# A two-layer hybrid decoder trunk: the pre-norm's factor moved behind the products, and transposed products turned to tokens on the partitions

## The chip, the core and the metric

One Trainium2 chip, one of its cores. The metric is the device time of one execution in microseconds (us). The kernel before took 1545.32 us, the median of 3 runs (1544.34 to 1547.5).

## What is computed

Two layers (D = 1024, 256 tokens, FFN width 2816) on a residual x in float32. Cut to what matters here:

```python
for l in range(DEPTH):
    x = x + 0.5 * rmsnorm(swiglu(rmsnorm(x, ffn1_pre_g[l]), w_ffn1_in[l], w_ffn1_out[l]), ffn1_post_g[l])
    h = rmsnorm(x, mix_pre_g[l])
    (z, xbc, dt_raw, rq, rk, rv, rg, aq, ak, av, gate) = split(h @ w_in[l])
    ys = [ssd_mixer(z, xbc, dt_raw, ...), retention_mixer(rq, rk, rv, rg, ...), swa_sink_attention(aq, ak, av, ...)]
    y = sum(sigmoid(gate + b_gate[l])[m] * (ys[m] @ w_branch[l, m]) for m in range(3)) @ w_out[l]
    x = x + rmsnorm(y, mix_post_g[l])
    x = x + 0.5 * rmsnorm(swiglu(rmsnorm(x, ffn2_pre_g[l]), w_ffn2_in[l], w_ffn2_out[l]), ffn2_post_g[l])
# rmsnorm(x, g) = x * rsqrt(mean(x * x) + EPS) * g; swiglu: silu(a) * b, then w_out
```

## The kernel before

Six phases run one after the other: FFN, mixer, FFN, for each layer. Every operand of a large product is held as two fp32r tiles, the rounded value (hi) and what is left (lo), and each product is three matmuls (`mm3`, lines 87 to 89): hi by lo, hi by hi, lo by hi. The weights are read in tiles of 128 x 1024 (512 KB, `raw`, 4 buffers) by SP's queue and split by ScalarE (hi, line 67) and VectorE (lo, line 68) into `hl`, 8 buffers, two of the eight 128-row blocks of a chunk in each; a chunk is 512 columns of a weight.

A product comes in two forms. `gemm` (line 91) keeps a block of the activations in TensorE, transposed (xT, yT, hT, with features on the partitions), and streams 512 columns of weights: the result has 128 tokens on the partitions. `gemmT` (line 100) keeps 128 columns of the weight and streams 256 tokens: the result has features on the partitions, which is how the next product wants it. It serves FFN chunks 2 to 10, the convolution's input `xbc`, the gates and the branch products. FFN chunks 0 and 1 use `gemm` and are transposed by TensorE.

Between two phases (a joint, in the prediction) `close` makes the last product for token tiles 0 and 1 (t = 0, 1), `postnorm` updates x, and `prenorm` opens the next phase: the sum of squares on ScalarE (line 135), two steps on GpSimd for the factor r (lines 126 and 128), xn = x * r * g on VectorE (line 161), eight transposes per tile (line 146) into PSUM (`pst`, 3 banks), and the split into hi and lo halves of xT. The engines run their queues in order; the order on each is set by the scheduler of the tile layer, from a model of its own of the times. Inside the mixer, `pump` hands out the small steps of attention, retention and the state-space scan between the products.

Of the kernel before, what the change touches and what calls it, by code (L numbers as in the profile page):

```python
# [11 lines left out]
ALU = mybir.AluOpType  # L12
# [27 lines left out]
class Trunk:  # L40
# [59 lines left out]
    def gemmT(self, ps, xT, slots, c0):  # L100
        """the transposed product: 128 columns of the weight from c0 on, by all tokens"""
        for k, (wh, wl) in enumerate(slots):
            x = xT[k // 2]
            cs = slice(c0, c0 + P)
            self.mm3(ps, wh[:, cs], wl[:, cs], x[:, k % 2, 0], x[:, k % 2, 1], k == 0, k == len(slots) - 1)

    def swiglu(self, a, b):
        nc = self.nc
        sl = self.t1([256], name="sl")
        nc.scalar.activation(out=sl, in_=a, func=AF.Silu)  # L110
        h = self.t1([256], name="h")
        nc.vector.tensor_tensor(out=h, in0=sl, in1=b, op=ALU.mult)  # L112
        return h
# [9 lines left out]
    def rstd(self, ss, eps):  # L123
# [143 lines left out]
    def begin(self, gname, l):  # L267
        """norm and transposes that open a phase: returns the tiles and what does one token tile"""
        g = self.gain(gname, l)
        xT = self.new_T(4, "xT")  # L270
        return xT, lambda t: self.prenorm(xT, t, g)
# [4 lines left out]
    def close(self, order, gemm, gpost, scale, nxt):  # L276
        """output projection, residual update and the next phase's opening, token tile by token tile"""
        y = {}
        for n, t in order:
            y[t, n] = gemm(n, t)  # L280
            if n:
                self.postnorm(t, [y[t, 0], y[t, 1]], gpost, scale, 4 * EPS, nxt is None)
                if nxt:
                    nxt(t)

    def ffn(self, i, l, xT, nxt):
        nc, A = self.nc, self.A
        w = A[f"w_ffn{i}_in"][l]
# [34 lines left out]
    def att_kv(self, t, ps):  # L323
# [22 lines left out]
    def att_q(self, g, t, ps):  # L346
# [3 lines left out]
        nc.scalar.activation(out=qn[:, :, 0], in_=ps, func=AF.Copy, scale=0.125)  # L350
        nc.vector.scalar_tensor_tensor(out=qn[:, :, 1], in0=ps, scalar=0.125, in1=qn[:, :, 0].bitcast(F32),
# [73 lines left out]
    def rotate(self, key, t, ps):  # L425
# [5 lines left out]
        nc.vector.tensor_tensor(out=a, in0=ps, in1=cs[:, 0].unsqueeze(1).unsqueeze(1).to_broadcast([P, 4, 2, 64]),  # L431
                                op=ALU.mult)
        for o in range(2):
            nc.vector.tensor_tensor(out=b[:, :, o], in0=ps[:, :, 1 - o],
                                    in1=cs[:, 1 + o].unsqueeze(1).to_broadcast([P, 4, 64]), op=ALU.mult)
# [75 lines left out]
    def silu2(self, ps, dtype=F32, name="gz"):  # L511
        """2 * silu of a PSUM bank, in a new SBUF tile"""
        nc = self.nc
        g = self.t2([512], name=name)
        nc.scalar.activation(out=g, in_=ps, func=AF.Tanh, scale=0.5)
        nc.vector.scalar_tensor_tensor(out=g, in0=g, scalar=1.0, in1=ps, op0=ALU.add, op1=ALU.mult)
        return g

# [37 lines left out]
    def conv(self, i, ps):  # L556
        nc, S = self.nc, self.S
        for j in range(2):
# [4 lines left out]
            p = ps[:, j]  # L563
# [11 lines left out]
    def ssd(self):  # L575
# [46 lines left out]
        for t in range(NT):  # L622
            y = xsd[t].rearrange("p h d -> p (h d)")
            for g in range(2):
# [31 lines left out]
                nc.vector.tensor_tensor(out=ys, in0=ys, in1=S.pop(f"z{g}{t}"), op=ALU.mult)  # L656
# [9 lines left out]
    def mixer_consts(self, l):  # L666
# [14 lines left out]
    def mix(self, l, xT, nxt):  # L681
# [4 lines left out]
        S = self.S = {}  # L686
# [6 lines left out]
        def kvdt(t):  # L693
            ps = self.gemm(xT, t, skv, 272)
            nc.vector.tensor_tensor(out=dtx[:, t], in0=ps[:, 256:272], in1=self.dtb, op=ALU.add)
            self.att_kv(t, ps)

        def main(key, t, slots):
# [4 lines left out]
            elif key[:2] == "rv":  # L703
                if n == 0:
                    S[f"rv{t}"] = self.t4([D], name="rv")
                self.copy(S[f"rv{t}"][:, 512 * n:512 * n + 512], ps)
                S[f"rv{n}{t}"] = True
            elif key[:2] == "rg":
                g = self.silu2(ps)
                nc.vector.tensor_tensor(out=g, in0=g, in1=gret[:, 512 * n:512 * n + 512], op=ALU.mult)  # L710
                S[f"rg{n}{t}"] = g
            elif key[0] == "z":
                S[f"z{key[1]}{t}"] = self.silu2(ps)
# [8 lines left out]
        S["dt"] = dtx  # L722
        main("aq0", 1, s0)
# [20 lines left out]
        acc = [self.t4([4, T], name="ysum") for n in range(2)]  # L744
        ysT = []
        for m, gens in ((2, att), (1, ret), (0, ssd)):
# [6 lines left out]
            gate = []  # L753
            for n in range(2):
                slots = W(ci)
                ci += 1
                for b in range(2):
                    ps = self.acc.tile([P, 2, T], F32, tag="acc", name="acc")
                    g = self.t2([2, T], name="gate")
                    for j in range(2):  # L760
                        c = 4 * n + 2 * b + j
                        self.gemmT(ps[:, j], xT, slots, (2 * b + j) * P)
                        nc.scalar.activation(out=g[:, j], in_=ps[:, j], func=AF.Tanh, scale=0.5,  # L763
                                             bias=self.bg[:, 8 * m + c:8 * m + c + 1])
                    gate.append(g)
                    self.pump()
                    if len(gate) == 2:
                        for gen in gens:
                            self.finish(gen)
                        yT = self.new_T(4, "yT")  # L770
                        for t in range(NT):
                            self.transposed(yT, S[f"y{m}{t}"], t)
            slots = sum((self.units(A["w_branch"][l], 4 * m + u) for u in range(4)), [])
            for i in range(4):
                ps = self.acc.tile([P, 2, T], F32, tag="acc", name="acc")
                for j in range(2):
                    self.gemmT(ps[:, j], yT, slots[8 * (i // 2):8 * (i // 2) + 8], (2 * (i % 2) + j) * P)
                g = gate[i]
                a = acc[i // 2][:, 2 * (i % 2):2 * (i % 2) + 2]
# [36 lines left out]
def host(inputs):  # L816
# [21 lines left out]
    out["b_gate"] = np.ascontiguousarray(f.pop("b_gate").reshape(DEPTH, 24, P).transpose(0, 2, 1))  # L838
# [6 lines left out]
def consts():  # L845
    """Tables that depend on the shapes alone."""
# [46 lines left out]
```

## Time and profile before

| | |
|---|---|
| runs | 1544.34, 1545.32, 1547.5 us |
| span of the profiled execution | 1548.9 us, 25438 instructions |
| the profiled execution's own time beside it | not recorded apart from the span |
| TensorE, weight loads | 98%, 90% of the span |
| VectorE, ScalarE, GpSimd | 63%, 49%, 3% |
| granted TensorE clock | 0.992 of 2.4 GHz over the span |
| DMA | 271.46 MB, mean 175 GB/s |

Engines in the rows: PE is TensorE, PEld its weight loads, DVE VectorE, ACT ScalarE, POOL GpSimd, SP the queue that issues transfers. Matmuls overlap and their ends are modelled, so the distance between starts says more than the duration; the number of weight loads in a stretch gives it. "[1.61 <-DVE xn]" is the idle time of the engine before the row, and what ended it.

### The profile page before, as it was taken

How to read it: one execution, taken by the hardware profiler on the slowest of the kernel's cores; microseconds unless marked ns; L12 is line 12 of the kernel's file. 1: busy time of each engine (PE TensorE's matmuls, PEld its weight loads, DVE VectorE, ACT ScalarE, POOL GpSimd, SP SyncE). 2: the span in 40 equal slices, each digit the busy share in tenths (PEclk: the TensorE clock that was granted, in tenths of full speed). 3: DMA queues.
4: the chain of work that ended last, by engine and by line, in shares of the span. 5: the costliest groups of instructions: out<-in, count | busy, mean ns of one | idle time of the engine just before them, and what ended most of it. 6: DMA issues, size and time to landing. Idle time of an engine off the chain costs nothing.

```text
span 1548.9 us, 25438 instructions
## 1 busy us (share of the span) xinstructions
PE 1516.6 (98%) x10122; PEld 1392.1 (90%) x10122; DVE 973.1 (63%) x1548; ACT 756.5 (49%) x1299; POOL 49.8 (3%) x72
## 2 busy tenths in 40 slices
PE   7999999999999999999999999999999999999998
PEld 5999878998989997999879998789989999789986
DVE  5554467788576666454564544777876776765553
ACT  6444456465445445454454543645545535554442
POOL 0000010001000001000010000100010000000000
PEclk9999999999999999999999999999999999999999
DMA  7555456535363546555555445654444545545452
GB/s 284 195 186 195 152 200 206 178 110 178 120 207 128 174 167 209 181 174 173 197 195 186 166 173 181 211 196 141 152 131 164 174 153 178 190 169 199 164 191 81
DMA packets 81111, 271.46 MB, mean 175 GB/s; under 512 B 10400, under 2 KB 15200, under 8 KB 80992
## 3 DMA queue, kind: packets, MB, share of 16 engines
q1 hardware_dynamic: 80992, 269.84, 51.3%
q8 instruction: 79, 1.29, 0.3%
q14 instruction: 40, 0.33, 0.1%
HBM read 268.73 MB, written 1.07 MB: 174 GB/s over the span
## 4 chain that ended last, share of the span: by engine, by line
PE 82%; issue 13%; DMA 1%; DVE 1%; ACT 1%; POOL 1%; SPq 0%; DVEq 0%; POOLq 0%; ACTq 0%
PE acc L87 23%; PE acc L89 23%; PE acc L88 23%; PE xbc L89 1%; PE xbc L87 1%; PE xbc L88 1%; PE po L416 1%; PE pT L146 1%; PE pS L383 1%; PE py L641 1%; DVE hl L68 1%; PE pb L408 1%; DMA raw<-w_ffn_in 1%; PE pb L634 0%; DMA gain<-ffn_pre_g 0%
## 5 line engine op out<-in xcount | busy, mean ns | idle before, releaser
L68 DVE TENSOR_TENSOR hl<-raw,hl 128x1024 fp32r<-128x1024 f32 (+2 forms) x544 | 583.4, 1104 | 291.1 <-ACT hl L67 285.4
L67 ACT CAST hl<-raw 128x1024 fp32r<-128x1024 f32 (+2 forms) x544 | 497.9, 952 | 326.3 <-PE acc L89 266.3
L87 PE MATMUL acc<-xT,hl 128*128 128x256 f32 x1536 | 435.8, 284 | 0.3 <-ACT gate L763 0.3
L89 PE MATMUL acc<-xT,hl 128*128 128x256 f32 x1536 | 435.8, 284 | 0.0
L88 PE MATMUL acc<-xT,hl 128*128 128x256 f32 x1536 | 435.4, 284 | 0.0
L87 PEld LDWEIGHTS acc<-xT,hl 128*128 128x128 f32 x1536 | 294.5, 192 | 2.0 <-issue 1.1
L88 PEld LDWEIGHTS acc<-xT,hl 128*128 128x128 f32 x1536 | 294.5, 192 | 0.6 <-issue 0.2
L89 PEld LDWEIGHTS acc<-xT,hl 128*128 128x128 f32 x1536 | 294.4, 192 | 0.2 <-issue 0.2
L87 PE MATMUL acc<-hl,xT 128*128 128x512 f32 (+1 forms) x480 | 192.1, 401 | 3.6 <-ACT xT L67 3.4
L88 PE MATMUL acc<-hl,xT 128*128 128x512 f32 (+1 forms) x480 | 188.7, 393 | 0.0
L89 PE MATMUL acc<-hl,xT 128*128 128x512 f32 (+1 forms) x480 | 186.2, 396 | 2.4 <-DVE xT L68 2.3
L87 PE MATMUL acc<-hl,hT 128*128 128x512 f32 x352 | 137.0, 389 | 0.0
L88 PE MATMUL acc<-hl,hT 128*128 128x512 f32 x352 | 137.0, 389 | 0.0
L89 PE MATMUL acc<-hl,hT 128*128 128x512 f32 x352 | 136.3, 389 | 0.0
L87 PEld LDWEIGHTS acc<-hl,xT 128*128 128x128 f32 x480 | 93.2, 194 | 22.2 <-ACT xT L67 5.5
L89 PEld LDWEIGHTS acc<-hl,xT 128*128 128x128 f32 x480 | 91.5, 192 | 23.6 <-DVE xT L68 6.0
L87 PE MATMUL acc<-yT,hl 128*128 128x256 f32 x384 | 109.5, 286 | 0.0
L88 PE MATMUL acc<-yT,hl 128*128 128x256 f32 x384 | 109.2, 285 | 0.0
L88 PEld LDWEIGHTS acc<-hl,xT 128*128 128x128 f32 x480 | 93.2, 194 | 17.4
L89 PE MATMUL acc<-yT,hl 128*128 128x256 f32 x384 | 108.2, 283 | 0.0
L112 DVE TENSOR_TENSOR h<-sl,acc 128x256 f32<-128x256 f32 x88 | 36.8, 418 | 85.5 <-ACT sl L110 85.2
L110 ACT ACTIVATE sl<-acc 128x256 f32<-128x256 f32 x88 | 33.5, 381 | 106.0 <-PE acc L89 105.5
(201 smaller groups left out, 1853.1 us busy)
## 6 DMA issues: line engine op xcount, KB each, us to landing
raw<-w_ffn_in SPq DMA_DIRECT2D x176, 512.0 KB, 4.7
raw<-w_main SPq DMA_DIRECT2D x152, 512.0 KB, 4.5
raw<-w_ffn_out SPq DMA_DIRECT2D x88, 512.0 KB, 4.8
raw<-w_branch SPq DMA_DIRECT2D x48, 512.0 KB, 4.6
raw<-w_out SPq DMA_DIRECT2D x16, 512.0 KB, 5.0
bias<-rows SPq DMA_DIRECT2D x8, 512.0 KB, 5.8
raw<-w_kvdt SPq DMA_DIRECT2D x8, 272.0 KB, 2.9
gain<-ffn_pre_g SPq DMA_DIRECT2D x4, 512.0 KB, 4.3
```

Source lines behind the costliest of these rows:

```text
L67: nc.scalar.copy(out=hi, in_=src)
L68: nc.vector.tensor_tensor(out=lo, in0=src, in1=hi.bitcast(F32), op=ALU.subtract)
L87: mm(ps, xh, wl, start=start, stop=False)
L88: mm(ps, xh, wh, start=False, stop=False)
L89: mm(ps, xl, wh, start=False, stop=stop)
L110: nc.scalar.activation(out=sl, in_=a, func=AF.Silu)
L112: nc.vector.tensor_tensor(out=h, in0=sl, in1=b, op=ALU.mult)
L146: nc.tensor.transpose(ps[:, j], src[:, (q + j) * P:(q + j + 1) * P], self.ident)
L383: nc.tensor.matmul(pS[:, i, :w], qT[t][:, hb + j + i], kT[:, g, hl, ks], start=hl == 0, stop=hl == 1)
L408: nc.tensor.transpose(pp[:, j], s[:, j, b * P:b * P + P], self.ident)
L416: nc.tensor.matmul(po[:, j], pT[b][:, j], vt[:, vo + b, 64 * g:64 * g + 64], start=b == 0, stop=b == t)
L641: nc.tensor.matmul(py[:, j], L[:, j], xdt[t][:, 8 * g + j], start=True, stop=True)
```

## The change

`prenorm` transposes x itself. The gain g is now one value per partition (a 128 x 8 tile `pg`, read in place of the broadcast row), applied as the blocks leave PSUM, one block of 128 columns at a time. The sum of squares and r come after that, beside the products, and r is applied where products leave PSUM: in `swiglu`, keys, values, queries (r8 = r/8), rotation, rv, rg and z (rh = r/2 inside tanh), dt, the gates; for the convolution, whose output has tokens along the row, a transposed row of r (`rT`) multiplies the PSUM bank first. FFN chunks 2 to 10, the gates and the branch products use `gemm`; what they give is transposed by TensorE (`h`, and the mixed sum `ysum`). The gates' biases become broadcast rows (`gain`, 512 KB for each mixer branch). The convolution's product stays `gemmT`.

```diff
-    def swiglu(self, a, b):
+    def swiglu(self, a, b, r):
...
-        nc.scalar.activation(out=sl, in_=a, func=AF.Silu)
+        nc.scalar.activation(out=sl, in_=a, func=AF.Silu, scale=r)
...
-        nc.vector.tensor_tensor(out=h, in0=sl, in1=b, op=ALU.mult)
+        nc.vector.scalar_tensor_tensor(out=h, in0=b, scalar=r, in1=sl, op0=ALU.mult, op1=ALU.mult)
...
-    def prenorm(self, xT, t, g):
+    def prenorm(self, xT, t, g, r):
...
-        r = self.rstd(self.sumsq([x[:, t, 0:512], x[:, t, 512:1024]], 1.0 / 32), EPS)
-        xn = self.t4([D], name="xn")
-        for i in range(2):
-            s = slice(512 * i, 512 * i + 512)
-            nc.vector.scalar_tensor_tensor(out=xn[:, s], in0=x[:, t, s], scalar=r, in1=g[:, s],
-                                           op0=ALU.mult, op1=ALU.mult)
-        self.transposed(xT, xn, t)
+        ts = slice(t * P, t * P + P)
+        for q in range(0, KD, 4):
+            ps = self.pst.tile([P, 4, P], F32, tag="pst", name="pT")
+            for j in range(4):
+                nc.tensor.transpose(ps[:, j], x[:, t, (q + j) * P:(q + j + 1) * P], self.ident)
+            for j in range(4):
+                k = q + j
+                hi, lo = xT[k // 2][:, k % 2, 0, ts], xT[k // 2][:, k % 2, 1, ts]
+                nc.scalar.activation(out=hi, in_=ps[:, j], func=AF.Copy, scale=g[:, k:k + 1])
+                nc.vector.scalar_tensor_tensor(out=lo, in0=ps[:, j], scalar=g[:, k:k + 1], in1=hi.bitcast(F32),
+                                               op0=ALU.mult, op1=ALU.subtract)
+        self.rstd(self.sumsq([x[:, t, 0:512], x[:, t, 512:1024]], 1.0 / 32), EPS, r)
...
-            if c < 2:
-                ps = self.gemm(xT, t, slots[c])
-                h = self.swiglu(ps[:, 0:256], ps[:, 256:512])
-                self.transposed(hT[c:c + 1], h, t)
-            else:
-                ps = self.acc.tile([P, 2, T], F32, tag="acc", name="acc")
-                for j in range(2):
-                    self.gemmT(ps[:, j], xT, slots[c], 256 * j + P * t)
-                h = self.swiglu(ps[:, 0], ps[:, 1])
-                self.split(hT[c][:, t, 0], hT[c][:, t, 1], h)
+            ps = self.gemm(xT, t, slots[c])
+            h = self.swiglu(ps[:, 0:256], ps[:, 256:512], r[t])
+            self.transposed(hT[c:c + 1], h, t)
...
+        pr = self.t2([2, T], name="pr")
+        nc.vector.tensor_tensor(out=pr, in0=ps, in1=S["rT"].unsqueeze(1).to_broadcast([P, 2, T]), op=ALU.mult)
...
+            bg = self.gain("b_gate", l, m * D)
...
+                for t in range(NT):
+                    ps = self.gemm(xT, t, slots)
+                    g = gate[n, t] = self.t2([512], name="gate")
+                    nc.vector.scalar_tensor_tensor(out=g, in0=ps, scalar=r[t], in1=bg[:, 512 * n:512 * n + 512],
+                                                   op0=ALU.mult, op1=ALU.add)
+                    nc.scalar.activation(out=g, in_=g, func=AF.Tanh, scale=0.5)
...
+            for n, t in order:
+                ps = self.gemm(yT, t, u[2 * n] + u[2 * n + 1])
...
+                    self.transposed(ysT[2 * n:2 * n + 2], a, t)
```

What this makes of the engines' order, at the two places that the prediction speaks of. In the names, `acc` is a product's PSUM bank, `hl` a weight tile, `h` the FFN's hidden values.

In TensorE's queue, FFN, between two halves of a chunk, before:

```order
L88 MATMUL acc_669<-xT_95,hl_665 128x256
L89 MATMUL acc_669<-xT_95,hl_665 128x256
L87 MATMUL acc_724<-xT_92,hl_650 128x256
L88 MATMUL acc_724<-xT_92,hl_650 128x256
L89 MATMUL acc_724<-xT_92,hl_650 128x256
```

and with the change, where h_656 is the second half of the chunk before, made of acc_629, which ended ahead of all 24 matmuls of acc_684:

```order
L88 MATMUL acc_684<-hl_680,xT_95 128x512
L89 MATMUL acc_684<-hl_680,xT_95 128x512
L87 MATMUL acc_718<-hl_665,xT_92 128x512
L88 MATMUL acc_718<-hl_665,xT_92 128x512
L89 MATMUL acc_718<-hl_665,xT_92 128x512
L147 MATMUL pT_658<-identr_86,h_656 128x128 x2
L87 MATMUL acc_718<-hl_665,xT_92 128x512
```

Operands have changed places, the shape has doubled, and two transposes stand three matmuls into the next half.

In VectorE's queue at the joint from the first FFN into the mixer, from the last output product (acc_1937) on, before (xT_1687 to 1690 are the four pairs of blocks of xT, pT_1919 and 1928 the transposes of token tile 0, yg the product by the post-norm's gain, the two writes of x_81 those of token tile 1):

```order
L171 TENSOR_TENSOR yg_2006<-acc_1937,gain_1565 128x512
L161 SCALAR_TENSOR_TENSOR xn_1916<-x_81,r_1914,gain_1685 128x512 x2
L68 TENSOR_TENSOR hl_2146<-raw_2144,hl_2146 128x1024
L68 TENSOR_TENSOR hl_2151<-raw_2149,hl_2151 128x1024
L68 TENSOR_TENSOR xT_1687<-pT_1919,xT_1687 128x2x128
L176 SCALAR_TENSOR_TENSOR x_81<-yg_2004,r_2015,x_81 128x512
L176 SCALAR_TENSOR_TENSOR x_81<-yg_2006,r_2015,x_81 128x512
L68 TENSOR_TENSOR xT_1688<-pT_1919,xT_1688 128x2x128
```

and with the change (xT_1319 to 1322 the pairs, pT_1541 and 1554 the transposes of tile 0, pT_1657 the first of tile 1):

```order
L178 TENSOR_TENSOR yg_1644<-acc_1575,gain_1197 128x512
L68 TENSOR_TENSOR hl_1793<-raw_1791,hl_1793 128x1024
L68 TENSOR_TENSOR hl_1798<-raw_1796,hl_1798 128x1024
L168 SCALAR_TENSOR_TENSOR xT_1319<-pT_1541,pg_1317,xT_1319 128x128
L183 SCALAR_TENSOR_TENSOR x_81<-yg_1642,r_1653,x_81 128x512
L183 SCALAR_TENSOR_TENSOR x_81<-yg_1644,r_1653,x_81 128x512
L168 SCALAR_TENSOR_TENSOR xT_1319<-pT_1541,pg_1317,xT_1319 128x128
L168 SCALAR_TENSOR_TENSOR xT_1320<-pT_1541,pg_1317,xT_1320 128x128
L168 SCALAR_TENSOR_TENSOR xT_1321<-pT_1554,pg_1317,xT_1321 128x128
L168 SCALAR_TENSOR_TENSOR xT_1319<-pT_1657,pg_1317,xT_1319 128x128
```

xn is gone, and one low half of tile 0 (half as wide as before) stands ahead of tile 1's writes of x. ScalarE's queue at the same joint, before:

```order
L67 CAST hl_2151<-raw_2149 128x1024
L135 ACTIVATE junk_2011,ss_2008<-acc_1937 128x512
L67 CAST xT_1687<-pT_1919 128x2x128
L67 CAST xT_1688<-pT_1919 128x2x128
L67 CAST xT_1689<-pT_1928 128x2x128
L135 ACTIVATE junk_2020,ss_2019<-x_81 128x512
L135 ACTIVATE junk_2022,ss_2019<-x_81 128x512
L67 CAST xT_1690<-pT_1928 128x2x128
```

and with the change:

```order
L67 CAST hl_1798<-raw_1796 128x1024
L167 ACTIVATE xT_1319<-pT_1541,pg_1317 128x128
L136 ACTIVATE junk_1649,ss_1646<-acc_1575 128x512
L167 ACTIVATE xT_1319<-pT_1541,pg_1317 128x128
L136 ACTIVATE junk_1684,ss_1683<-x_81 128x512
L136 ACTIVATE junk_1686,ss_1683<-x_81 128x512
L167 ACTIVATE xT_1320<-pT_1541,pg_1317 128x128
```

Two of tile 0's eight blocks, in place of six, stand ahead of the squares of tile 1's x (junk from x_81).

## Rows read from the trace of the kernel before

**Rows 1.** The page, busy time: us, share of the span, instructions

```profile
PE 1516.6 (98%) x10122; PEld 1392.1 (90%) x10122; DVE 973.1 (63%) x1548; ACT 756.5 (49%) x1299; POOL 49.8 (3%) x72
```

**Rows 2.** Windows: us, then busy us (instructions) by engine, clock, DMA

```profile
60.00:140.00 80.00, 80.00 (x669) 80.00 (x668) 43.02 (x56) 37.49 (x56) 0.00 (x0) 1.00 0.50 180
155.00:200.00 45.00, 45.00 (x200) 37.28 (x199) 20.77 (x23) 17.70 (x25) 0.00 (x0) 1.00 0.50 165
```

**Rows 3.** Groups: engine, operation, out<-in, shapes, count | busy, mean ns | idle

```profile
L87 PE MATMUL acc<-xT,hl 128*128 128x256 f32 x1536 | 435.8, 284 | 0.3 <-ACT gate L763 0.3
L87 PE MATMUL acc<-yT,hl 128*128 128x256 f32 x384 | 109.5, 286 | 0.0
```

**Rows 4.** Timeline of TensorE: start us, us, instruction; eight transposes

```profile
1364.29 0.39 PE L88 MATMUL acc<-hl,xT 128*128 128x512 f32 x1
1364.51 0.39 PE L89 MATMUL acc<-hl,xT 128*128 128x512 f32 x1
1364.75 1.03 PE L146 MATMUL pT<-identr,xn 128*128 128x128 f32 x8
1365.54 0.48 PE L89 MATMUL acc<-hl,xT 128*128 128x512 f32 x1
1365.85 0.40 PE L87 MATMUL acc<-hl,xT 128*128 128x512 f32 x1
```

**Rows 5.** Windows of 18 us at three joints, instructions that touch acc

```profile
583.00:601.00 18.00, 13.92 (x46) 10.38 (x46) 1.10 (x2) 1.07 (x3) 0.81 0.66 226
777.00:795.00 18.00, 12.87 (x43) 9.78 (x43) 1.11 (x2) 1.07 (x3) 0.81 0.62 206
1348.90:1366.90 18.00, 12.35 (x51) 9.21 (x51) 1.11 (x2) 1.23 (x4) 1.00 0.53 196
```

**Rows 6.** Timeline, all engines, at the joint into the mixer; last row at 1357

```profile
205.95 0.39 PE L89 MATMUL acc<-hl,hT 128*128 128x512 f32 x1
...
207.94 1.05 ACT L67 CAST hl<-raw 128x1024 fp32r<-128x1024 f32 x1 [0.84 <-DMA raw<-w_main]
...
207.95 1.29 PE L146 MATMUL pT<-identr,xn 128*128 128x128 f32 x8 [1.61 <-DVE xn L161]
...
208.38 2.36 DVE L68 TENSOR_TENSOR hl<-raw,hl 128x1024 fp32r<-128x1024 f32 x2
...
208.89 0.59 ACT L135 ACTIVATE junk<-acc 128x512 bf16<-128x512 f32 x1
...
209.67 1.23 POOL L126 TENSOR_SCALAR v<-ss 128x1 f32<-128x1 f32 x1 [2.65 <-DVE hl L68]
...
209.89 0.39 PE L87 MATMUL acc<-hl,xT 128*128 128x272 f32 x1 [0.65 <-ACT xT L67]
...
210.99 0.56 POOL L128 TENSOR_TENSOR r<-v,mhalf 128x1 f32<-128x1 f32 x1
...
211.58 1.42 DVE L176 SCALAR_TENSOR_TENSOR x<-yg,r,x 128x512 f32<-128x512 f32 x2 [0.51 <-POOL r L128]
...
1356.44 1.42 DVE L176 SCALAR_TENSOR_TENSOR x<-yg,r,x 128x512 f32<-128x512 f32 x2 [0.84 <-POOL r L128]
```

**Rows 7.** Timeline of the start

```profile
9.29 1.41 DVE L161 SCALAR_TENSOR_TENSOR xn<-x,r,gain 128x512 f32<-128x512 f32 x2 [4.16 <-DMA gain<-ffn_pre_g]
...
10.47 1.14 ACT L67 CAST hl<-raw 128x512 fp32r<-128x512 f32 x2 [5.00 <-DMA raw<-w_ffn_in]
```

**Rows 8.** Groups of evacuating instructions

```profile
L110 ACT ACTIVATE sl<-acc 128x256 f32<-128x256 f32 x88 | 33.5, 381 | 106.0 <-PE acc L89 105.5
L783 DVE SCALAR_TENSOR_TENSOR gate<-gate,acc 128x512 f32<-128x512 f32 x16 | 11.0, 684 | 5.1 <-PE acc L89 5.1
L332 ACT CAST kh<-acc 128x128 fp32r<-128x128 f32 x8 | 2.1, 265 | 9.9 <-DVE dtx L695 9.9
L504 DVE SCALAR_TENSOR_TENSOR rt<-po,mv,gz 128x256 f32<-128x256 f32 x16 | 7.0, 475 | 0.0
```

**Rows 9.** Window over projections, attention and convolution of the first mixer

```profile
280.00:400.00 120.00, 120.00 (x848) 111.82 (x848) 95.30 (x212) 63.49 (x128) 6.64 (x4) 1.00 0.43 141
```

More of the change, by code (lines that the diff above doesn't have):

```diff
@@ L267, in begin @@
     def begin(self, gname, l):
-        g = self.gain(gname, l)
+        g = self.sm.tile([P, KD], F32, tag="pg", name="pg", bufs=2)
+        self.nc.sync.dma_start(out=g, in_=self.A[gname][l])
         xT = self.new_T(4, "xT")
-        return xT, lambda t: self.prenorm(xT, t, g)
+        r = [self.sm.tile([P, 1], F32, tag=f"pr{t}", name="pr", bufs=2) for t in range(NT)]
+        return (xT, r), lambda t: self.prenorm(xT, t, g, r[t])
     def ffn_out_slots(self, i, l):
@@ L349, in att_q @@
         qn = self.t4([8, 2, 64], R, "qn")
-        nc.scalar.activation(out=qn[:, :, 0], in_=ps, func=AF.Copy, scale=0.125)
-        nc.vector.scalar_tensor_tensor(out=qn[:, :, 1], in0=ps, scalar=0.125, in1=qn[:, :, 0].bitcast(F32),
+        r = S["r8"][t]
+        nc.scalar.activation(out=qn[:, :, 0], in_=ps, func=AF.Copy, scale=r)
+        nc.vector.scalar_tensor_tensor(out=qn[:, :, 1], in0=ps, scalar=r, in1=qn[:, :, 0].bitcast(F32),
                                        op0=ALU.mult, op1=ALU.subtract)
@@ L509, in ret, with silu2 @@
             S[f"y1{t}"] = y
-    def silu2(self, ps, dtype=F32, name="gz"):
+    def silu2(self, ps, rh, name="gz"):
         nc = self.nc
         g = self.t2([512], name=name)
-        nc.scalar.activation(out=g, in_=ps, func=AF.Tanh, scale=0.5)
+        nc.scalar.activation(out=g, in_=ps, func=AF.Tanh, scale=rh)
         nc.vector.scalar_tensor_tensor(out=g, in0=g, scalar=1.0, in1=ps, op0=ALU.add, op1=ALU.mult)
@@ L685, in mix @@
         self.gssd = self.gain("ssd_norm_g", l)
-        S = self.S = {}
+        xT, r = xT
+        S = self.S = {"r": r}
+        r8, rh = ([self.small(1, f"{n}{t}") for t in range(NT)] for n in ("r8", "rh"))
+        for t in range(NT):
+            for o, c in ((r8, 0.125), (rh, 0.5)):
+                nc.gpsimd.tensor_scalar(out=o[t], in0=r[t], scalar1=c, scalar2=None, op0=ALU.mult)
+        S["r8"] = r8
         att, ret, ssd = [self.att(g) for g in range(2)], [self.ret()], [self.ssd()]
@@ L705, in main @@
                     S[f"rv{t}"] = self.t4([D], name="rv")
[L706 removed]
+                o = S[f"rv{t}"][:, 512 * n:512 * n + 512]
+                if n:
+                    nc.scalar.activation(out=o, in_=ps, func=AF.Copy, scale=r[t])
+                else:
+                    nc.vector.tensor_scalar(out=o, in0=ps, scalar1=r[t], scalar2=None, op0=ALU.mult)
                 S[f"rv{n}{t}"] = True
             elif key[:2] == "rg":
[L709 to L710 removed]
+                g = self.silu2(ps, rh[t])
+                nc.vector.scalar_tensor_tensor(out=g, in0=g, scalar=r[t], in1=gret[:, 512 * n:512 * n + 512],
+                                               op0=ALU.mult, op1=ALU.mult)
                 S[f"rg{n}{t}"] = g
             elif key[0] == "z":
[L713 removed]
+                S[f"z{key[1]}{t}"] = self.silu2(ps, rh[t])
             else:
@@ L722, in mix @@
         S["dt"] = dtx
+        pr = self.pbank()
+        for t in range(NT):
+            nc.tensor.transpose(pr[:, t], r[t].to_broadcast([P, P]), self.ident)
+        S["rT"] = self.sm.tile([P, T], F32, tag="rT", bufs=1, name="rT")
+        self.copy(S["rT"], pr[:, 0:2].rearrange("p t n -> p (t n)"))
         main("aq0", 1, s0)
@@ L743, in mix @@
                 main(key, t, slots)
-        acc = [self.t4([4, T], name="ysum") for n in range(2)]
-        ysT = []
+        acc = [self.t4([D], name="ysum") for t in range(NT)]
+        ysT = self.new_T(4, "ysT")
         for m, gens in ((2, att), (1, ret), (0, ssd)):
@@ L752, in mix @@
                         main(key, t, slots)
-            gate = []
+            bg = self.gain("b_gate", l, m * D)
+            gate = {}
             for n in range(2):
@@ L756, in mix @@
                 ci += 1
[L757 to L765, printed above, removed]
-                    self.pump()
[L767 to L779, printed above, removed]
+                for t in range(NT):
+                    ps = self.gemm(xT, t, slots)
+                    g = gate[n, t] = self.t2([512], name="gate")
+                    nc.vector.scalar_tensor_tensor(out=g, in0=ps, scalar=r[t], in1=bg[:, 512 * n:512 * n + 512],
+                                                   op0=ALU.mult, op1=ALU.add)
+                    nc.scalar.activation(out=g, in_=g, func=AF.Tanh, scale=0.5)
+                    self.pump()
@@ new lines, in mix @@
+                if n == 0:
+                    for gen in gens:
+                        self.finish(gen)
+                    yT = self.new_T(4, "yT")
+                    for t in range(NT):
+                        self.transposed(yT, S[f"y{m}{t}"], t)
+            u = [self.units(A["w_branch"][l], 4 * m + i) for i in range(4)]
+            order = [(n, t) for n in range(2) for t in range(NT)] if m else [(n, t) for t in range(NT) for n in range(2)]
+            for n, t in order:
+                ps = self.gemm(yT, t, u[2 * n] + u[2 * n + 1])
+                g = gate[n, t]
+                a = acc[t][:, 512 * n:512 * n + 512]
@@ L837, in host @@
     out["w_conv"] = np.ascontiguousarray(cw.reshape(DEPTH, 5, 12, P).transpose(0, 3, 2, 1))
-    out["b_gate"] = np.ascontiguousarray(f.pop("b_gate").reshape(DEPTH, 24, P).transpose(0, 2, 1))
+    for n in ("ffn1_pre_g", "mix_pre_g", "ffn2_pre_g"):
+        out[n] = np.ascontiguousarray(f.pop(n).reshape(DEPTH, KD, P).transpose(0, 2, 1))
     out.update(f)
```

38 lines of the change are left out of this document (20 added, 18 removed).

## The prediction

> **What bounds the kernel now.** I read the page first: TensorE is busy 98% of the span, VectorE 63%, ScalarE 49% [rows 1]. A busy TensorE here can still be slow TensorE, so the next view is the count of weight loads in two undisturbed stretches of the first FFN [rows 2]: 668 in 80 us where the products run transposed (256 columns each) is 119.8 ns apiece, 199 in 45 us of the output projection (512 columns each) is 226.1 ns. Two short products cost 239.6 ns, one long one of the same columns 226.1. Then the instruction groups give how many of the short ones there are [rows 3]: 1536 for each of lines 87 to 89 on xT and 384 for each on yT, 5760 in all (the 576 of the convolution stay short in both kernels). Last I read the joints between phases, where TensorE does wait [rows 5, 6].
>
> **The product itself.** The change turns the 5760 into 2880 of 512 columns: 5760 x 0.1198 = 690.0 us become 2880 x 0.2261 = 651.2, **-38.8 us**, all on the path. The same columns stream either way; what is saved is 6.75 ns for each of the short ones. The Trainium skill (TensorE: Matmul & The Clock Gate, section Back-to-back issue gap) puts a warm matmul at its columns over 2.4 GHz plus 2.5 ns; by that estimate 256 columns take 109.2 and 512 take 215.8 ns, the halving brings only 7 us, and my sum would end near +18 us, slower. Both measured pitches lie over the page's, the short one by more in proportion, so I go by [rows 2].
>
> **New transposes.** FFN chunks 2 to 10 now come out with tokens on the partitions and are transposed: 9 chunks x 2 token tiles x 2 blocks x 4 FFNs = 144; the mixed sum adds 16 per layer, the row of factors 2 per layer: 180. From the matmul before a group of eight to the second matmul after it, 1364.51 to 1365.85, are 1.34 us [rows 4]; less two matmuls of 0.226 that is 0.111 us each. 180 x 0.111 = **+20 us**. That none of them waits: in TensorE's order the transposes of a chunk's half stand 23 to 27 matmuls after that half's product, 5.2 us or more. They need Silu (0.38 us), the product on VectorE (0.48 at most, as line 504's form) [rows 8] and two hand-overs, some 1.3 us, plus at worst one weight split on each engine ahead of them (1.05 and 1.2) [rows 6]. If this cover were gone, each microsecond late would cost 72 us, once per half chunk.
>
> **The start.** The gain of the first norm (512 KB) is no longer ahead of the weights. VectorE waited 4.16 us for it and wrote xn at 9.29, the first weights could be cast at 10.47 [rows 7]. Without it the weights land at least those 1.2 us sooner, and the transposes of x no longer wait for xn. I take **-2 us**; bounds 0, if the transfers behind eat it up, and -4.
>
> **The joints.** The diff takes the factor r out of the transposes' way, which looks like a shorter chain: sum of squares, GpSimd's two steps and the scaling by r and g (xn) no longer stand between x and the transposes. But what counts is the order on the engines. Before, the five joints lose: 18 us of window less 46, 43 and 51 matmuls of 0.226 and 16 transposes of 0.111 leave 5.8, 6.5 and 4.7 us [rows 5]; into the mixer, waits of 1.61 and 0.65 [rows 6], a smaller third one and the tails of the matmuls ahead of them make about 3.5, twice. Together 24, of which about 6 are matmuls at the lower of the two clock levels, 1.2 GHz, after the idle time (mean granted 0.81 in two of the windows, 1.00 in the third).
> Now the joint into the mixer as the new order has it, from the end of the last product at 206.2 (call it 0), with durations of [rows 6, 8]. TensorE does the eight transposes of tile 0 to 0.9. ScalarE's last weight cast waits for its transfer and ends at 2.8, the first high half (one block of 128 columns now; 0.27 as line 332's cast, which I raise to 0.36 for the scale that is read per partition) at 3.2, the square of tile 1's product (0.59) with the reading of its sum at 3.95, the second high half at 4.3. GpSimd takes 1.23 + 0.56 to 5.9, VectorE writes x of tile 1 until 6.7 and 7.3. In TensorE's order four transposes of tile 1 stand right behind the second high half, so they wait from 5.5 until 6.7; on VectorE every low half but the first stands behind both writes of x, and on ScalarE every further high half behind both squares of that x, at 8.3 (before, a pair of low halves and three of the four high pairs stood ahead). The third block's product starts at 8.7, the last four transposes end about 12. In these 12 us TensorE has 16 transposes (1.8) and 14 products of each width (4.9): 5.3 lost, where it was 3.5. For the joints behind the output projection of the mixer the same walk, with x of tile 1 complete at 1357.86 [rows 6], 9.0 after the end, gives 4.3, for that between two FFNs 4.2. Sum 2 x 5.3 + 2 x 4.3 + 4.2 = 23, plus the same 6 for the clock: 29, so **+5 us**. Bounds: -12 (all joints like the shortest wait seen, 2.5) and +16 (clock at the lower level in all five).
>
> **VectorE in the mixer.** It gains the gates' factor and bias (24 of 512 elements, 0.68 each as line 783's) [rows 8] and the scaling ahead of the convolution (12 of the same size): 24 us over both layers, where it is busy 95.3 of 120 us in the fullest stretch [rows 9]. That leaves room, so I take **+2** for local collisions; bounds 0 and 24. Everything else trades like for like: scaled copies for copies, h's split from PSUM instead of SBUF, 6 gain loads dropped and 6 loads of gate biases added. SP issues those behind weights that are three chunks ahead of TensorE; each waits for the buffer of the gain before, free when the last chunk's evacuation is done, and a few us there are covered by those chunks.
>
> **Sum.** -38.8 + 20 - 2 + 5 + 2 = -14 us. The profiled execution spans 1548.9; the trace shows nothing around that span, and the median of the runs, 1545.3, is 3.6 below it, so the change is taken from the median: **1531 us**. What a measurement of this kernel can tell from no change is about 0.2%, 3 us.
>
> **Rivals.**
> - The joints do get shorter: x is ready for tile 0 before the last product ends (-3.5 in the mixer's joint), and the orders lose less than I count since neighbours run ahead. For it: the norm's chain of two squares, two GpSimd steps and xn is gone from the tile's path, and with less idle time the clock would stay at 2.4 GHz. Against: the order puts tile 1's chain ahead of tile 0's halves. At -12 instead of +5: 1514.
> - VectorE becomes the bound in the mixer, at the gates and the convolution: the weight splits queue behind the new instructions and TensorE waits for weights. Price 24 instead of 2, **1553, slower**. It decides from the point at which VectorE's busy share there passes what its neighbours' waits leave, near full; 95.3 of 120 plus some 5 in that stretch speaks against it.
> - The long products don't keep their pitch in the chunks, where casts and splits write SBUF beside them, and cost twice the short ones: the 38.8 are gone, **1570, slower**. Against it: chunks 0 and 1 of each FFN already run this form, and in [rows 4] (1364.29 to 1364.51) it steps 0.22 to 0.23 us. The page's rule above, that only columns count, lands on this side too.
>
> **How the numbers follow.** Forecast with its own bounds, 1521 to 1542: 0.62. Short joints: 0.2. VectorE as the bound: 0.08. Columns alone: 0.03. The rest, 0.07, is a sum of joints and collisions at their worse bounds, around 1545. The range of 8 in 10 takes in most of the short joints and stops short of the two slow rivals: 1516 to 1546. Faster by over 0.2% (under 1542.2): 0.62 + 0.2 and a little of the rest, 0.85; within 0.2%: 0.07; slower: 0.08.
>
> **What would show it.** Right: 7422 matmuls on TensorE in the new profile (10122 - 2880 + 180), 226 to 227 ns per load in an FFN chunk, transposes of h with no idle time before them, idle time at the joints that ends with x or with a high or low half of xT, first product near 10 us. Wrong: idle TensorE in the chunks that ends with h or with hl, a pitch of 240 in the chunks, or a joint under 3 us with the clock at its upper level throughout.

## The result, and the profile after

The changed kernel takes 1538.7 us, the median of four runs (1538.08 to 1538.96), beside 1544.9 of the kernel before in the same comparison: the recorded ratio is 0.9941, interval 0.9925 to 0.9958, which is not the quotient of these two medians (0.9960). A second comparison in more rounds (below, a0_again) gave 0.9937 (0.9924 to 0.9951), with 1539.07 beside 1548.27. The change is worth -6 to -10 us; forecast was -14, and the time lies in the range. The profiled executions stand further apart, 1548.9 and 1536.3 us of span; single times of the kernel before lie up to 7 us apart (1545.5 to 1552.4 in b0_again). Where traces are compared below, they are these two, so the terms add up to some -12.6 and not to -6 to -10.

The page of the changed kernel, busy time by engine, answers to [rows 1]:

```profile
PE 1503.4 (98%) x7422; PEld 1257.9 (82%) x7422; DVE 1008.9 (66%) x1615; ACT 788.0 (51%) x1332; POOL 44.3 (3%) x80
```

The matmuls are the 7422 that were forecast. Windows show where the time went. First the kernel before, cut at the end of the last product of each phase (FFN, mixer, FFN; twice). Columns: us, then busy us (instructions) of PE, PEld, DVE, ACT, POOL, granted clock, DMA share, GB/s:

```profile
0.00:206.34 206.34, 194.75 (x1250) 176.61 (x1250) 110.34 (x152) 101.13 (x158) 3.58 (x13) 0.99 0.58 202
206.34:583.18 376.84, 374.01 (x2564) 344.92 (x2564) 273.63 (x491) 195.13 (x363) 16.88 (x18) 1.00 0.50 166
583.18:777.21 194.03, 191.89 (x1249) 175.50 (x1248) 107.08 (x143) 92.29 (x148) 5.29 (x8) 0.98 0.55 187
777.21:971.88 194.67, 191.46 (x1248) 175.47 (x1248) 104.83 (x137) 88.87 (x139) 4.40 (x9) 0.98 0.54 182
971.88:1349.01 377.13, 375.14 (x2565) 346.18 (x2564) 274.87 (x490) 193.80 (x361) 15.15 (x18) 1.00 0.49 166
1349.01:1548.94 199.93, 189.34 (x1248) 173.45 (x1248) 102.34 (x135) 85.23 (x134) 4.48 (x9) 0.99 0.48 165
```

The same windows of the changed kernel:

```profile
0.00:201.70 201.70, 192.80 (x856) 157.65 (x857) 113.44 (x155) 106.17 (x166) 3.57 (x13) 0.99 0.62 204
201.70:583.02 381.32, 374.50 (x2016) 320.43 (x2014) 287.82 (x519) 200.58 (x364) 13.57 (x23) 0.99 0.52 169
583.02:770.83 187.81, 186.87 (x846) 152.93 (x846) 108.79 (x147) 96.72 (x155) 5.04 (x7) 1.00 0.57 187
770.83:960.46 189.63, 187.70 (x854) 153.94 (x853) 107.39 (x141) 94.64 (x147) 4.49 (x9) 1.00 0.55 183
960.46:1340.91 380.45, 374.70 (x2016) 320.36 (x2014) 288.34 (x519) 200.18 (x363) 13.57 (x23) 0.99 0.52 169
1340.91:1536.30 195.39, 186.85 (x844) 152.61 (x843) 103.14 (x137) 89.68 (x140) 4.11 (x8) 1.00 0.49 163
```

The four FFNs gain 4.6, 6.2, 5.0 and 4.5 us, 20 in all. Both mixers, which were to gain 15.5 us on their products less 4 for 36 new transposes, lose 4.5 and 3.3. What TensorE waits for in the changed kernel, the four largest (engine line waited for: us in total, times, longest us):

```profile
PE acc L87 <- ACT xT L167: 7.6, 6, 2.2
PE pT L147 <- DVE prev L208: 5.0, 2, 2.5
PE pT L163 <- DVE identr L225: 4.7, 1, 4.7
PE pT L147 <- DVE h L113: 2.4, 1, 2.4
```

The first and third lines are the joints and the start. The fourth, once, is the first h of the kernel. The second is new, once in each mixer. `pT` there is the transposed output of the attention, `prev` a copy out of a PSUM bank by VectorE that has nothing to do with it. The timeline around it in the first mixer (start us, us, instruction, idle time before it and what ended it):

```profile
398.94 2.72 DVE L788 SCALAR_TENSOR_TENSOR gate<-acc,pr,gain 128x512 f32<-128x512 f32 x4
399.24 1.88 PE L630 MATMUL pp<-xdd,bn 128*128 128x512 f32 x4
400.96 0.64 PE L147 MATMUL pT<-identr,oatt 128*128 128x128 f32 x4
401.57 1.22 DVE L68 TENSOR_TENSOR hl<-raw,hl 128x1024 fp32r<-128x1024 f32 x1
402.70 0.76 DVE L504 BATCH_NORM_STATS2 st<-po 128x6 f32<-128x256 f32 x2
403.37 0.68 DVE L208 COPY prev<-pp 128x512 f32<-128x512 f32 x1
404.11 0.68 PE L147 MATMUL pT<-identr,oatt 128*128 128x128 f32 x4 [2.51 <-DVE prev L208]
405.23 1.12 PE L147 MATMUL pT<-identr,oatt 128*128 128x128 f32 x4 [0.45 <-DVE rt L514]
...
406.80 0.80 PE L87 MATMUL acc<-hl,yT 128*128 128x512 f32 x1 [0.46 <-ACT yT L67]
407.39 0.63 PE L88 MATMUL acc<-hl,yT 128*128 128x512 f32 x1
407.82 0.63 PE L87 MATMUL acc<-hl,yT 128*128 128x512 f32 x1
```

The three banks for transposes (`pst`) hold two `pp`, which are products of the state-space scan, and a product `po` of the retention. VectorE does four gates in a row, a weight split and two statistics before it empties the second `pp`. Afterwards the products step 0.43 us instead of 0.227, ten of them: the lower clock level. Take the distances between TensorE's starts, less the median distance of each form, and call their sum the excess. It is 9.5 and 8.5 us inside the two mixers, without the 16 us after each joint; before it was 2.0 and 1.5.

### The profile page after: what moved, and what is told of

The parts are those of the page before. It is cut to its first block, busy times and chain, and to the rows that moved or that the text cites. A ratio compares the mean times of both kernels' runs of the same rounds, so it can differ in the third digit from the quotient of the medians.

```text
span 1536.3 us, 20168 instructions
## 1 busy us (share of the span) xinstructions
PE 1503.4 (98%) x7422; PEld 1257.9 (82%) x7422; DVE 1008.9 (66%) x1615; ACT 788.0 (51%) x1332; POOL 44.3 (3%) x80
## 4 chain that ended last, share of the span: by engine, by line
PE 81%; issue 13%; DVE 2%; DMA 2%; ACT 1%; POOL 1%; SPq 0%; DVEq 0%; POOLq 0%; ACTq 0%
PE acc L87 23%; PE acc L89 23%; PE acc L88 22%; PE pT L147 2%; PE xbc L87 2%; PE xbc L88 2%; PE xbc L89 2%; PE po L422 1%; PE py L653 1%; PE pS L389 1%; DVE hl L68 1%; PE pb L414 1%; DMA raw<-w_main 1%; DMA raw<-w_ffn_in 1%; ACT hl L67 1%
## 5 line engine op out<-in xcount | busy, mean ns | idle before, releaser
L68 DVE TENSOR_TENSOR hl<-raw,hl 128x1024 fp32r<-128x1024 f32 (+2 forms) x544 | 594.3, 1106 | 220.4 <-ACT hl L67 202.9
L67 ACT CAST hl<-raw 128x1024 fp32r<-128x1024 f32 (+2 forms) x544 | 511.6, 956 | 272.8 <-PE acc L89 208.6
L87 PE MATMUL acc<-hl,xT 128*128 128x512 f32 (+1 forms) x1248 | 492.6, 395 | 9.5 <-ACT xT L167 7.6
L88 PE MATMUL acc<-hl,xT 128*128 128x512 f32 (+1 forms) x1248 | 487.2, 391 | 0.0
L89 PE MATMUL acc<-hl,xT 128*128 128x512 f32 (+1 forms) x1248 | 485.8, 394 | 1.0 <-DVE xT L168 1.0
L87 PEld LDWEIGHTS acc<-hl,xT 128*128 128x128 f32 x1248 | 236.0, 189 | 57.4 <-ACT xT L167 10.9
L89 PEld LDWEIGHTS acc<-hl,xT 128*128 128x128 f32 x1248 | 234.7, 189 | 49.3 <-DVE xT L168 3.2
L88 PEld LDWEIGHTS acc<-hl,xT 128*128 128x128 f32 x1248 | 236.1, 189 | 45.4
L113 DVE SCALAR_TENSOR_TENSOR h<-acc,pr,sl 128x256 f32<-128x256 f32 x88 | 42.1, 480 | 123.8 <-ACT sl L111 123.8
L111 ACT ACTIVATE sl<-acc,pr 128x256 f32<-128x256 f32 x88 | 41.8, 477 | 142.0 <-PE acc L89 137.8
L87 PE MATMUL acc<-hl,yT 128*128 128x512 f32 x192 | 77.3, 404 | 0.9 <-ACT yT L67 0.9
L89 PEld LDWEIGHTS acc<-hl,hT 128*128 128x128 f32 x352 | 66.1, 188 | 13.8
L88 PEld LDWEIGHTS acc<-hl,hT 128*128 128x128 f32 x352 | 66.1, 188 | 13.7
L87 PEld LDWEIGHTS acc<-hl,hT 128*128 128x128 f32 x352 | 66.1, 188 | 13.4
L88 PE MATMUL acc<-hl,yT 128*128 128x512 f32 x192 | 76.9, 402 | 0.0
L89 PE MATMUL acc<-hl,yT 128*128 128x512 f32 x192 | 75.0, 397 | 0.0
L87 PE MATMUL xbc<-xT,hl 128*128 128x256 f32 x192 | 55.8, 291 | 0.0
L67 ACT CAST hT<-pT 128x256 fp32r<-128x256 f32 x88 | 32.6, 373 | 45.2 <-PE pT L147 45.0
L89 PE MATMUL xbc<-xT,hl 128*128 128x256 f32 x192 | 55.0, 286 | 0.0
```

The costliest lines, as they stand in the source:

```text
L67: nc.scalar.copy(out=hi, in_=src)
L68: nc.vector.tensor_tensor(out=lo, in0=src, in1=hi.bitcast(F32), op=ALU.subtract)
L87: mm(ps, xh, wl, start=start, stop=False)
L88: mm(ps, xh, wh, start=False, stop=False)
L89: mm(ps, xl, wh, start=False, stop=stop)
L111: nc.scalar.activation(out=sl, in_=a, func=AF.Silu, scale=r)
```

## The experiments

Ratios are to the kernel before on the chip of the group, whose medians were 1547.8 to 1550.6 there; 0.001 is 1.55 us.

**b0_again and a0_again: both kernels once more.**

> The kernel before, unchanged, to have its profile beside the others of this group. Its profiled span was 1548.9 us, 3.6 above the median of its runs, that of the changed kernel 1536.3, 2.4 below its median: the profiles stand 12.6 apart, the medians 6.2. If the first profile was only an execution with more time at 1.2 GHz behind the joints, the new span is near 1543 and the joints lose some 5 us less than the 24 to 25 of the first one. If the difference is in how a profile is taken, the span comes out at 1549 again.

The span was 1547.4 (ratio 1.0007, interval 0.9996 to 1.0018): near the first profile, not 1543. By the excess the joints lost 25.7 us where they had lost 26.0, so the first profile was no exception; it is the median of the first four times of the kernel before, 1544.9, that lies lower than the median of any later group.

> The changed kernel, unchanged, timed in more rounds beside the kernel before on the chip of this group: the first comparison gave 0.9941 with an interval of 0.9925 to 0.9958, its two profiles stood 12.6 us apart and its medians 6.2. If the profiles are right about the change, the ratio is 0.992 or a little under it; if the first medians are, 0.996.

0.9937 (0.9924 to 0.9951), between the two, and neither 0.992 nor 0.996 is inside the interval.

**e1_ffn_alone: the FFN chunks alone.**

```diff
-            if c < 2:
...
-                    self.gemmT(ps[:, j], xT, slots[c], 256 * j + P * t)
...
+            ps = self.gemm(xT, t, slots[c])
+            h = self.swiglu(ps[:, 0:256], ps[:, 256:512])
+            self.transposed(hT[c:c + 1], h, t)
```

> The kernel before with only the FFN chunks 2 to 10 with tokens on the partitions; norm, gates and branches as before. Products: 3456 x 0.1198 become 1728 x 0.2261, -23.3 us; 144 transposes x 0.111, +16.0; together -7.3. Theory (from the two traces): nothing waits in the chunks, so -7 us against the kernel before, about 0.995 of it. Rival: the hand-over over ScalarE, VectorE and the transposes costs something per half chunk that the row factor hides in the changed kernel; at 0.1 us for each of 72 the gain would be gone.

0.9962 (0.9950 to 0.9973), -5.9 us. The term holds: TensorE waits for an `h` once in the whole kernel, 0.9 us, as it does in the kernel before.

**e2_gates_alone: gates and branches alone** (the loop of the changed kernel, its gate being a sum from PSUM).

```diff
-                        nc.scalar.activation(out=g[:, j], in_=ps[:, j], func=AF.Tanh, scale=0.5,
-                                             bias=self.bg[:, 8 * m + c:8 * m + c + 1])
+                    nc.vector.tensor_tensor(out=g, in0=ps, in1=bg[:, 512 * n:512 * n + 512], op=ALU.add)
+                    nc.scalar.activation(out=g, in_=g, func=AF.Tanh, scale=0.5)
```

> The kernel before with only gates and branches with tokens on the partitions (bias added by VectorE from PSUM, Tanh on ScalarE behind it, the sum transposed); norm and FFNs as before. Products: 2304 x 0.1198 become 1152 x 0.2261, -15.5 us; 32 transposes x 0.111, +3.6; together -12. Theory from the new trace: this part brings the stall in front of the first branch (6 us in each layer, with some ten matmuls at 1.2 GHz behind it), so 0 to +1 us against the kernel before. The prediction's term (+2 us for local collisions on VectorE) says -10.

0.9886 (0.9870 to 0.9903), -17.7 us; both forecasts missed, that from the traces by its sign too. There is no stall here (mixers 3.0 and 3.1 us of excess). Unlooked for, the joints behind the output projection fell from 4.6 and 5.0 to 2.5 and 2.7. In the kernel before TensorE waits there for xn (first fence, b0_again, start us, us, instruction); here the eight transposes follow with no idle time (second fence, e2_gates_alone):

```profile
583.15 1.32 PE L146 MATMUL pT<-identr,xn 128*128 128x128 f32 x8 [1.44 <-DVE xn L161]
```

```profile
577.25 1.03 PE L146 MATMUL pT<-identr,xn 128*128 128x128 f32 x8
```

The spans differ by 14.1, 3.6 less than the ratio says. The profiled execution (1535.08 us) was the longest of four, 3.3 above their median, so the trace can't show where the rest lies.

**e3_norm_back: the norm ahead of the transposes again, all else as changed.**

```diff
+        rs = self.rstd(self.sumsq([x[:, t, 0:512], x[:, t, 512:1024]], 1.0 / 32), EPS)
...
+        self.transposed(xT, xn, t)
...
-        r = [self.sm.tile([P, 1], F32, tag=f"pr{t}", name="pr", bufs=2) for t in range(NT)]
+        r = [self.one for t in range(NT)]
```

> The changed kernel with the norm put back ahead of the transposes (gain loaded over all partitions, xn, pairs of blocks split; the factors that are applied to PSUM are there but 1). Theory from the traces: the joints lost 24.9 us before and lose some 16 to 19 now, and the start came 4.6 earlier, so +9 to +11 us against the changed kernel, near 1549. The prediction's terms (joints +5, start -2, both undone): -3 us, near 1536.

0.9978 (0.9968 to 0.9987), +6.3 us against the changed kernel: the norm's move is a gain, as the traces have it and the prediction had not, though less than the traces' sum. By the excess it is 2.5 us at the joints (19.1 beside 16.6) and 3.9 in the first 30 us. The stall is still there (5.0 us in two waits for prev), and e2_gates_alone, whose mixer has no factor, has none. So not the moved norm but what the factor does in the mixer brings it.

**e4_conv_from_psum: less the convolution's factor.**

```diff
-        nc.vector.tensor_tensor(out=pr, in0=ps, in1=S["rT"].unsqueeze(1).to_broadcast([P, 2, T]), op=ALU.mult)
...
-            p = pr[:, j]
+            p = ps[:, j]
```

> The kernel of e3_norm_back (factors are 1) without the six products by the row of factors in each mixer: the convolution reads PSUM as before. VectorE is busy 19.5 and 16.5 of 20 us in the two stretches ahead of the stall in front of the first branch (360 to 400 us), and the wait of TensorE there ends with a copy of prev that stands late in VectorE's queue. Theory: those products (0.68 us each) fill VectorE, the queue runs late, and without them the stall and the ten slow matmuls go: -10 to -13 us against e3_norm_back (1545), near 1534. Rival: the gates' own products by factor and bias make it late, or the order, whatever the convolution does: no change, 1543 to 1546.

0.9875 (0.9858 to 0.9893), -16 us against e3_norm_back (the spans differ by 12.4). Twelve instructions of 0.68 us, 8.2 in all, on an engine that is not the bound cost 1.5 to 2 times their own time. The stall is gone, and the rival falls: the gates' factor and bias are still there.

**e5_more_banks, e6_prev_on_act, e8_transposes_first: three ways at the stall in the changed kernel.**

```diff
-        self.acc = pool("acc", 5, space=bass.MemoryType.PSUM)
-        self.pst = pool("pst", 3, space=bass.MemoryType.PSUM)
+        self.acc = pool("acc", 4, space=bass.MemoryType.PSUM)
+        self.pst = pool("pst", 4, space=bass.MemoryType.PSUM)
```

> The changed kernel with four PSUM banks for transposes and the like and four for the products, instead of three and five. The transposes of the attention's output wait 2.5 us until prev has been copied out of its bank. Theory that the bank decides: the wait goes, and with it the slow matmuls behind it, -8 to -12 us against the changed kernel (1538.7), 1527 to 1531. Rival, VectorE's queue itself: the split of yT stands in the same late queue, so the wait only moves to it, -2 us at most; with one bank fewer for the products these may also wait for their evacuation, slower.

0.9859 (0.9840 to 0.9877), -12 us: the bank theory's price, though a product then waits 2.0 us for VectorE elsewhere in each mixer. The waits for prev are gone.

```diff
-            self.copy(prev[:, g], ps)
+            nc.scalar.copy(out=prev[:, g], in_=ps)
```

> The changed kernel with both copies of prev on ScalarE (one of two was on VectorE); three banks as before. Theory: the stall ahead of the first branch hangs on this one copy, which stands behind four gates, a weight split and two statistics in VectorE's queue and holds the bank that the transposes need; ScalarE is free there, so the 2.5 us wait goes and most of the slow matmuls behind it: -6 to -12 us against the changed kernel. Rival: the next tile in a late queue (the split of yT, a read of the retention's product) takes its place: 0 to -3.

0.9922 (0.9909 to 0.9935), about -2, and not told apart from nothing. The rival holds; TensorE's rows of that place in e6_prev_on_act:

```profile
401.60 0.66 PE L147 MATMUL pT<-identr,oatt 128*128 128x128 f32 x4 [0.35 <-ACT prev L632]
404.28 0.70 PE L147 MATMUL pT<-identr,oatt 128*128 128x128 f32 x4 [2.03 <-DVE rt L514]
```

The copy is out of the way, and the same transposes wait for the next bank, the retention's.

```diff
+            if m == 2:
+                for gen in gens:
+                    self.finish(gen)
+                yT = self.new_T(4, "yT")
+                for t in range(NT):
+                    self.transposed(yT, S[f"y{m}{t}"], t)
             for n in range(2):
...
-                if n == 0:
+                if n == 0 and m != 2:
```

> The changed kernel with the attention finished and its output transposed ahead of the gate products of the first branch in the program. In TensorE's order the transposes still come behind all four gate products, but now ahead of the products that fill the three banks (statistics of the retention, prev), and the first branch product stands right behind them. If only the banks are at fault: the stall goes, -10 to -12 us against the changed kernel, near 1527. If it is that no product is left behind the transposes: TensorE waits for the halves of yT instead (they stand behind four gates in VectorE's queue), 2 to 4 us in each mixer are left, and the slow matmuls may stay: -3 to -7, 1532 to 1536.

0.9895 (0.9878 to 0.9912), -6.5 us. Banks are not all of it: waits for halves of yT stay (0.53, 0.46 and 0.80 us in the first mixer). The products behind them run at 2.4 GHz again.

What tells three of the cases apart is how many products TensorE has left. Windows of the products' instructions alone (columns as above), from the first `pp` to the last of those transposes, in the changed kernel, then e4_conv_from_psum, then e5_more_banks:

```profile
399.24:406.79 7.55, 0.00 (x0) 0.00 (x0) 2.42 (x4) 0.00 (x0) 0.86 0.66 236
```

```profile
390.28:399.30 9.02, 7.45 (x26) 4.93 (x27) 0.75 (x1) 0.00 (x0) 1.00 0.43 130
```

```profile
394.49:402.00 7.51, 5.10 (x19) 3.43 (x19) 1.39 (x2) 0.00 (x0) 1.00 0.24 79
```

None, 26 and 19. In the changed kernel all four gate products are done by then, and nothing covers a late bank. And VectorE is no fuller there than where this stall is gone. The stretch from 360 to 410 us, which holds the start of the branch in both, of the changed kernel and then of e5_more_banks:

```profile
360.00:380.00 20.00, 20.00 (x93) 16.55 (x93) 19.46 (x42) 9.73 (x14) 1.78 (x2) 1.00 0.56 181
380.00:400.00 20.00, 20.00 (x96) 16.57 (x95) 16.49 (x26) 11.45 (x16) 2.59 (x2) 1.00 0.59 189
400.00:410.00 10.00, 6.59 (x23) 4.30 (x22) 6.68 (x17) 4.60 (x11) 0.69 (x1) 0.73 0.46 162
```

```profile
360.00:380.00 20.00, 20.00 (x94) 16.64 (x93) 19.84 (x32) 11.55 (x16) 5.82 (x3) 1.00 0.56 171
380.00:400.00 20.00, 20.00 (x94) 16.05 (x93) 17.85 (x35) 10.64 (x17) 0.69 (x1) 1.00 0.51 174
400.00:410.00 10.00, 10.00 (x53) 8.53 (x52) 7.50 (x14) 5.12 (x12) 0.00 (x0) 1.00 0.65 209
```

So VectorE's load does not decide by itself. What is left is the order of the two queues with three banks between them. That is read from the traces and shown in part: e8_transposes_first keeps the three banks, changes the order, and takes off about half of what the fourth bank does. In e5_more_banks bank and order changed together, so how its 12 us divide between them is open. Why the order comes out so when the queues are built was not tried.

**f5_both_forms, f6_factor_in_ffn, f7_mixed_banks: what is best.** f5 is e1 and e2 together, on the kernel before. f7 is f6 with four and four PSUM banks. f6 gives the FFNs of f5, and only them, the factor behind the products:

```diff
+        if gname != "mix_pre_g":
...
+            return (xT, r), lambda t: self.prefactor(xT, t, g, r[t])
         g = self.gain(gname, l)
```

> The kernel before with FFN chunks, gates and branches with tokens on the partitions, and the norm as it was (no factor on PSUM anywhere). If the two parts add up: 0.9962 and 0.9886 give 0.985, near 1525. If each is only good with slack that the other one uses: between 1530 and 1537. It would beat both kernels in the first case.

> f5_both_forms with the row factor in the FFNs alone (there Silu and one product of VectorE take it in); the mixer keeps its norm ahead of the transposes. Theory from the traces: the start comes 4 to 5 us earlier, and the joints into the three later FFNs lose 7 to 10 us less, -11 to -15 against f5_both_forms, near 1512. The prediction's walk through the joints (4.3, 4.2, 4.3 lost instead of 5.8, 6.5, 4.7) and its start say -6: 1519.

> f6_factor_in_ffn (0.9817) with four and four PSUM banks. In f6 the stall ahead of the first branch is gone already, so if the banks only helped there: no change, 1520 to 1523. If the products miss the fifth bank (in e5_more_banks one waited 2.0 us for VectorE in each mixer): 2 to 6 us slower. If the mixer's transposes wait for banks elsewhere: 2 to 4 faster.

f5 0.9865 (0.9848 to 0.9882): the parts add up but for 2.6 us (0.9848 by the sum). f6 0.9817 (0.9800 to 0.9833), -7.4 against f5, nearer to the prediction's walk than to the traces' sum. f7 0.9812 (0.9799 to 0.9826), no different from f6, so the fourth bank gains nothing where the stall is not: 1519.65 us, 29 below the kernel before beside it.

## Why the prediction was right, and where it was not

The sign and the range held; of five terms three were near and two far off, in opposite directions. By the two profiled executions of the result (they lie 3 to 6 us further apart than the medians, as said above):

| term | predicted | measured |
|---|---|---|
| products and new transposes | -38.8 + 20 | -16.9 |
| start | -2 | -3.5 |
| joints | +5 | -9.3 |
| VectorE in the mixer | +2 | +14.5 |
| inside the FFNs, tail | 0 | +2.5 |
| sum | -14 | -12.7 (spans: -12.6) |

The other two traces, b0_again and a0_again, give -10.4 for the joints and +12.3 for VectorE in the mixer.

**Products and transposes.** Right. The 2880 step 227 ns, and the first row is the sum of each form's count by its median step. By the formula that the Trainium skill (TensorE: Matmul & The Clock Gate, section Back-to-back issue gap) gives for a warm matmul by itself the halving would have brought 7 us only, an estimate; the trace does not agree, and e1_ffn_alone (-5.9) would by that formula be slower, its 144 transposes being 16 us.

**The start.** Right in kind: the first transposes stand at 4.66, where by the profile they wait for the identity, instead of at 10.10, where they waited for xn [rows 7] (first row before, second after), -5.4, and of this 1.9 are lost again in waits of the first 30 us, above all the 2.42 for the first h.

```profile
10.10 1.97 PE L146 MATMUL pT<-identr,xn 128*128 128x128 f32 x8 [10.10 <-DVE xn L161]
4.66 1.97 PE L163 MATMUL pT<-identr,x 128*128 128x128 f32 x8 [4.66 <-DVE identr L225]
```

**The joints.** The failed step is the hand walk, "the order puts tile 1's chain ahead of tile 0's halves", with "the same 6 for the clock". Into the mixer it was close: 4.7 and 4.9 of excess (5.3 walked). Behind the output projections and between the FFNs it gave 4.2 to 4.3 where 1.9, 2.3 and 2.8 are lost, and the 6 us at 1.2 GHz are gone from these three, whose windows answer to [rows 5] with the clock at 1.00 in each (in a0_again too):

```profile
583.00:601.00 18.00, 16.21 (x69) 12.23 (x68) 1.56 (x3) 1.52 (x4) 1.00 0.47 160
770.80:788.80 18.00, 14.81 (x61) 11.06 (x61) 1.66 (x3) 1.63 (x4) 1.00 0.50 174
1340.90:1358.90 18.00, 15.76 (x68) 11.83 (x66) 1.56 (x3) 1.52 (x4) 1.00 0.39 129
```

46, 43 and 51 products are now 69, 61 and 68. A joint under 3 us with the clock at its upper level is a sign that the prediction had named for being wrong. The clock now falls behind both joints into the mixer; their windows, first two before, then two after:

```profile
206.20:224.20 18.00, 13.45 (x70) 10.33 (x70) 1.44 (x4) 2.38 (x8) 1.00 0.50 184
971.70:989.70 18.00, 13.98 (x65) 10.77 (x64) 1.44 (x4) 2.17 (x7) 0.91 0.51 180
201.70:219.70 18.00, 13.94 (x70) 11.14 (x69) 1.63 (x4) 2.46 (x7) 0.91 0.42 154
960.50:978.50 18.00, 13.90 (x67) 11.06 (x68) 1.60 (x4) 2.08 (x6) 0.91 0.57 191
```

What the walk had wrong behind the output projections can be read at the second of them, which ends at 1340.91:

```profile
1336.88 1.03 PE L163 MATMUL pT<-identr,x 128*128 128x128 f32 x8
1343.10 0.50 PE L87 MATMUL acc<-hl,xT 128*128 128x512 f32 x1 [0.84 <-ACT xT L167]
1347.35 0.74 DVE L183 SCALAR_TENSOR_TENSOR x<-yg,r,x 128x512 f32<-128x512 f32 x1
```

The transposes of tile 0 stand 4.0 us ahead of the end, and x of tile 1 is complete 7.2 us after it (6.7 at the first output projection), where the walk took 9.0 from the kernel before.

This was the rival "the joints do get shorter" (-12, a chance of 0.2), but the norm's move is only part of it. e2_gates_alone shortens the two joints behind the output projections by 4.4 with the norm left where it was. e3_norm_back, with the new layout and the old place of the norm, loses 2.5 and 2.8 there and 5.7 between the FFNs; the changed kernel loses 1.9, 2.3 and 2.8. So behind the output projections nearly all came with the layout, and between the FFNs it came with the norm's move. How the layout does it was not tried.

**VectorE in the mixer.** The failed step is "that leaves room, so I take +2". The new instructions were counted nearly right (14 us more of busy VectorE in each mixer by the windows; 12 predicted), and the bound of 24 held. But the rival "VectorE becomes the bound in the mixer" had the wrong mechanism: it looked for weights that come late, from a busy share near full. No product waits for hl inside the mixers. It was a PSUM bank read late, at the one place where TensorE's order has no product left.

The two errors, 14 one way and 12.5 the other, made a sum that looks well judged and was not: that it came so near is luck.

## What to carry to other kernels

Where added work goes on an engine that is not the bound, ask not only how full that engine is but which PSUM banks it empties, who needs them next, and how many products stand behind the one that would wait. An edit that does two things is worth splitting: here the token layout alone is worth 21 us (f5), and the factor behind the products 7 more in the FFNs, while the same factor in the mixer's convolution costs 12 to 16 (e4 against e3). A fourth bank for the short-lived tiles (e5) bought back 12, with the order of the queues changed along with it.

## Not expected of the hardware

Ten products behind 3.4 us of waits (2.51, 0.45, 0.46) with only transposes between them ran at 1.2 GHz, 0.43 us a step. In e8_transposes_first three waits of 0.46 to 0.80 us near each other, with products between, were followed by none.
